# Weight sums of the HGRN's value product: eight VectorE operations replaced by fourteen adding transfers from GpSimd's queue

## The chip, the cores and the metric

The kernel runs on one core of a Trainium2 chip. The metric is the device time of one execution in microseconds. Three runs of the kernel before took 1425.98, 1425.44 and 1424.23 us, median 1425.44 us. Besides these there is one profiled execution, from which all rows of the profile come.

## The reference

A decoder trunk of two layers over 512 tokens of width 1024, in float32. Layer 0 mixes tokens with a Mamba-2 block, layer 1 with an HGRN2 block; after each mixer come a normalisation, a squared-ReLU MLP, a second normalisation and a gated embedding. The change lies at the border of the two layers: the last part of layer 0 and the first product of layer 1.

```
h = layer_norm(ALPHA * x + mix, ...)
h = layer_norm(ALPHA * h + sq_relu_mlp(h, w1, w2), ...)
x = h + sigmoid(h @ ple_w_gate) * (p @ ple_w_proj)
...
q, fz, v, g = split(x @ w_in, 4)      # HGRN2 of layer 1
```

The product that the change is about makes half of the columns of `v` and `g` from `x` and the matching half of the weights.

## The kernel before

**How a product is made.** Each float32 operand is split into a rounded part `hi` and the rest `lo`, and a product takes three matmuls (`mm3`: hi by hi, hi by lo, lo by hi). A weight unit is 128x1024, 512 KB. `unit` loads it into one of three `raw` buffers, `split` makes `whi` (a cast on ScalarE, L113) and `wlo` (a subtraction on VectorE, L115); there are six buffers of each. A `raw` buffer is free for the next load when its `wlo` is done.

**Block products.** The MLP's second product and the first HGRN product multiply 2x2 blocks with seven block products in place of eight. For four of the seven the weight is a sum of blocks, `t1` to `t4`, each of two units. `weight_sums` loads blocks from HBM into eight buffers `r` (L321, on SyncE's queue) and makes sums in place on VectorE (L327 `t3`, L329 `t1`, L330 `t2`, L333 `t4`), two of each per call. In this scheme the sums are, with blocks w11 to w22 of the weights: t3 = w22 - w12, t1 = w12 - w11, t2 = t3 + w11, t4 = w21 - t2.

**The stage around the change.** `mlp_and_gate(0, ...)` ends with the last group of block products (the seven products run in the order a11, s3, s2, a22, s1, a12, s4). After the fifth of them two row chunks of the accumulator are normalised (`layer_norm`: row mean L212, squares on ScalarE L215, L218, square root L219, reciprocal L221, and the two passes L223 and L224 on VectorE), after the seventh the other two. `transpose_split` then transposes each chunk on TensorE (L233, two groups of four transposes a chunk into one PSUM bank `pt`) and evicts it (L237 on ScalarE, L238 on VectorE). The gate's product follows, with weights `wp` (one unit, the projection) and `wg` (four units) for each half, and its own transposes for the next layer (L448, L451 to L453).

`values4` is the first product of the HGRN. Its weight sums are asked for at its beginning, with a priority that puts their instructions ahead in the queues (`VALUE_SUMS`); its matmuls run after the gate's. It uses t3, then t2, t4 and t1. The data side of the blocks is made by `put` on ScalarE and VectorE; the results are drained from PSUM by `first` (a copy on ScalarE) and `more` (an addition on VectorE) into `res`.

**What sets the order.** A scheduler gives each engine one fixed order of instructions from priorities and its own estimates; in `values4` and the HGRN TensorE's order is the written one. SyncE's queue issues in order: each load waits for its buffer, and all loads behind it wait too. Before the change GpSimd issues no transfers and does a few memsets, the last of them (in the line after `scbs`) for the HGRN's score tiles.

Of the kernel before, what the change touches and what calls it, by code (L numbers as in the profile page):

```python
# [11 lines left out]
AF = mybir.ActivationFunctionType  # L12
ALU = mybir.AluOpType
PSUM = bass.MemoryType.PSUM

P = 128
# [18 lines left out]

JOBS = "q2 q3 q4 q5 v2 q6 q7 v3 o".split()
FILL = (2.94, 1.03, 1.27, 1.83, 2.22)
VALUE_SUMS = 60
AHEAD = 6.0
LAST = 0.78  # L40
CONSTS = dict(ident=P, triu=P, eps=1, convw=96, convb=24, dskip=16, snw=16, dtc=2, hlb=8, hnw=1)
# [3 lines left out]
def trunk(ctx: ExitStack, tc, a):  # L45
    nc = tc.nc
# [21 lines left out]
    def mk(p, shape, tag, dt=F32, **kw):  # L68
        return p.tile(list(shape), dt, tag=tag, name=nm(tag), **kw)

    def f32(t):
        return t.bitcast(F32)
# [16 lines left out]
    def tmp(tag, shape, dt=F32):  # L89
        return mk(phase[0], shape, tag, dt, bufs=phase[2].get(tag, 1))  # L90

    def bank(p, tag):
        return mk(p, [P, T], tag)
# [8 lines left out]
    def unit(src, lead=LEAD):  # L102
        n = src.shape[1]
        with tc.high_priority(offset=lead):
            raw = mk(raws, [P, 1024], "raw")
            nc.sync.dma_start(raw[:, :n], src)
        return split(raw[:, :n], lead)

    def split(f, lead=LEAD):
        n = f.shape[1]  # L110
        with tc.high_priority(offset=lead):
            hi = mk(whip, [P, 1024], "whi", F32R)
            nc.scalar.copy(hi[:, :n], f)  # L113
            lo = mk(wlop, [P, 1024], "wlo", F32R)
            nc.vector.tensor_sub(lo[:, :n], f, f32(hi[:, :n]))  # L115
        return hi, lo

    def mm3(out, sh, sl, mh, ml, start, stop, **kw):
        nc.tensor.matmul(out, sh, mh, start=start, stop=False, **kw)  # L119
        nc.tensor.matmul(out, sh, ml, start=False, stop=False, **kw)  # L120
        nc.tensor.matmul(out, sl, mh, start=False, stop=stop, **kw)  # L121
# [26 lines left out]
    with tc.high_priority(offset=FIRST):  # L148
        idle = tmp("sq", [P, T])
        nc.vector.memset(idle, 0.0)  # L150
        ps = bank(psm, "pm")
# [163 lines left out]
    def weight_sums(w, lead, eng=nc.vector):  # L315

        t = [[None, None] for _ in range(4)]

        def load(i, u, src):
            t[i][u] = tmp("r", [P, 1024])  # L320
            nc.sync.dma_start(t[i][u], src)  # L321

        with tc.high_priority(offset=lead):
            for u in range(2):
                load(0, u, w[0][1][u])
                load(2, u, w[1][1][u])
                eng.tensor_sub(t[2][u], t[2][u], t[0][u])  # L327
                load(1, u, w[0][0][u])
                eng.tensor_sub(t[0][u], t[0][u], t[1][u])  # L329
                eng.tensor_add(t[1][u], t[2][u], t[1][u])  # L330
            for u in range(2):
                load(3, u, w[1][0][u])
                eng.tensor_sub(t[3][u], t[3][u], t[1][u])  # L333
        return t
# [171 lines left out]
    def values4(xs, rows, late):  # L506

        w = [[[a["whvg"][4 * j + 2 * i + u] for u in range(2)] for j in range(2)] for i in range(2)]
        t1, t2, t3, t4 = weight_sums(w, VALUE_SUMS, nc.vector)
        a11, a12, a21, a22 = (rows[i][:, j] for i in range(2) for j in range(2))  # L510
        res = [[mk(w4, [P, 2, T], "ab"[i]) for i in range(2)] for _ in range(2)]

        def put(f):
            t = mk(b8, [P, 2, 4, 256], "b8", F32R)
            nc.scalar.copy(t[:, 0], f)
            nc.vector.tensor_sub(t[:, 1], f, f32(t[:, 0]))
            return lambda k, c: tuple(t[:, i, k, c * P : (c + 1) * P] for i in range(2))

        def part(i, j):
            sl = lambda c: slice((2 * i + c) * P, (2 * i + c + 1) * P)  # L520
            return lambda k, c: (xs.h(4 * j + k, sl(c)), xs.l(4 * j + k, sl(c)))

        def product(x, us, banks, start, drain):
            for c in range(2):
                for k in range(4):
                    hi, lo = us[k // 2]
                    ks = slice(k % 2 * T, (k % 2 + 1) * T)
                    mm3(banks[c], *x(k, c), hi[:, ks], lo[:, ks], start and k == 0, k == 3, skip_group_check=True)
                with tc.high_priority(offset=SOON):
                    drain(c, banks[c])  # L530

        def first(i, j):
            return lambda c, ps: nc.scalar.copy(res[j][i][:, c], ps)

        def more(i, j):
            return lambda c, ps: nc.vector.tensor_add(res[j][i][:, c], ps, res[j][i][:, c])

        pair = lambda: [bank(psj, "pj") for _ in range(2)]
        sums = lambda t: [split(v) for v in t]
        x, z, y = [bank(psy, "py%d" % c) for c in range(2)], pair(), pair()  # L540
        with tc.high_priority(offset=EARLY):
            nc.vector.tensor_sub(a11, a11, a21)
            s3 = put(a11)
        product(part(0, 0), [unit(v) for v in w[0][0]], x, True, first(0, 0))
        for f in late:
            f()
        product(part(0, 1), [unit(v) for v in w[1][0]], z, True, more(0, 0))
        nc.vector.tensor_add(a21, a21, a22)
        nc.vector.tensor_sub(a22, a22, a11)
        s2 = put(a22)  # L550
        product(s3, sums(t3), y, True, first(1, 1))
        s1 = put(a21)
        product(s2, sums(t2), x, False, first(1, 0))
        nc.vector.tensor_sub(a12, a12, a22)
        s4 = put(a12)
        product(part(1, 1), sums(t4), y, False, more(1, 0))
        product(s1, sums(t1), x, False, more(1, 1))
        product(s4, [unit(v) for v in w[1][1]], x, False, first(0, 1))
        for j in range(2):
            for i in range(2):  # L560
                g = res[j][i][:, :, 256:]
                nc.scalar.activation(g, g, AF.Silu)
            made["vg", j] = res[j]


    ps = bank(psj, "pj")
    first = [bank(psy, "py0"), bank(psy, "py1"), bank(psj, "pj"), bank(psj, "pj")]
    for k in range(8):
# [10 lines left out]
        parts = [[v[:, k % 2, i * P : (i + 1) * P] for v in four[k // 2]] for i in range(4)]  # L579
# [203 lines left out]
    for j in range(17):  # L783
# [6 lines left out]
        if pend is not None:  # L790
            i = j - 1
# [7 lines left out]
            w = snw[:, i : i + 1]  # L799
# [16 lines left out]
    with tc.manual_schedule(engines={mybir.EngineType.PE}):  # L816
        values4(x_s, rows, late)
# [286 lines left out]
    with tc.manual_schedule(engines={mybir.EngineType.PE}):  # L1104
        for h in range(0, 8, 2):
# [5 lines left out]
            scale = 1.0 if h < 6 else LAST  # L1111
# [129 lines left out]
```

## Time and profile before

| | us |
|---|---|
| median of three runs | 1425.44 |
| the profiled execution | 1424.0 |
| its span on the core | 1422.2 |
| TensorE busy | 1412.7 |
| VectorE busy | 1055.1 |
| ScalarE busy | 754.2 |
| GpSimd busy | 1.9 |

Times in the rows are microseconds from the start of the span. A row of a group gives line, engine, operation, output and inputs, count, busy time and the mean of one in ns, then idle time before it and what ended it. A row of the timeline gives start, length, engine, line, operation, count and, in square brackets, how long the engine was idle before and what released it. `raw<-in_w` is a load into a raw buffer, `r<-in_whvg` a load for the sums of `values4`.

### The profile page before, as it was taken

The page shows a single profiled execution, that of the slowest core. Times are in us where ns is not written, and L with a number is a line of the kernel's source. Part 1 is how long each engine was busy: PE and PEld are TensorE (multiplying, and loading weights), DVE is VectorE, ACT ScalarE, POOL GpSimd, SP SyncE. Part 2 cuts the span into 40 slices and gives each one's busy share as a digit, 9 for nine tenths or more (in the row PEclk, how much of TensorE's full clock was granted, in tenths as well). Part 3 has the DMA queues.
Part 4 walks back from the last instruction along what each step waited for, and adds up shares of the span by engine and source line. Part 5 has one row for each costly group of instructions (what it writes and reads, how often), then busy time and mean ns, then how long its engine had stood idle before and what let it go on. Part 6 is the DMA issues. An engine that isn't in the chain of part 4 may idle for free.

```text
span 1422.2 us, 20042 instructions
## 1 busy us (share of the span) xinstructions
PE 1412.7 (99%) x7869; PEld 1172.5 (82%) x7869; DVE 1055.1 (74%) x1736; ACT 754.2 (53%) x1134; POOL 1.9 (0%) x12
## 2 busy tenths in 40 slices
PE   9999999999999999999999999999999999999998
PEld 7888888888888888888888888877898888888887
DVE  8998687797966767677986576678695867667873
ACT  7776454563265454545545556655555444544641
POOL 0000000000000000000000000000000000000000
PEclk9999999999999999999999999999999999999999
DMA  8432323233333434344621421222163444434231
GB/s 313 138 124 90 120 87 121 102 115 127 145 119 120 161 133 149 133 146 166 214 83 49 133 90 60 75 90 90 46 236 104 148 140 142 149 133 163 89 119 45
DMA packets 49390, 178.00 MB, mean 125 GB/s; under 512 B 5520, under 2 KB 6288, under 8 KB 49168
## 3 DMA queue, kind: packets, MB, share of 16 engines
q1 hardware_dynamic: 49296, 176.73, 36.3%
q8 instruction: 62, 1.02, 0.3%
q14 instruction: 32, 0.26, 0.1%
HBM read 174.54 MB, written 2.16 MB: 124 GB/s over the span
## 4 chain that ended last, share of the span: by engine, by line
PE 94%; DVE 2%; ACT 2%; DMA 1%; issue 0%; ACTq 0%; DVEq 0%
PE pj L119 24%; PE pj L120 24%; PE pj L121 24%; PE py L119 5%; PE py L121 5%; PE py L120 5%; PE py L735 1%; PE pt L233 1%; PE py L741 1%; PE pm L705 1%; DMA raw<-in_wssd 1%; PE py L972 1%; PE pt L693 1%; PE py L1078 1%; DVE wlo L115 0%
## 5 line engine op out<-in xcount | busy, mean ns | idle before, releaser
L113 ACT CAST whi<-raw 128x1024 fp32r<-128x1024 f32 x222 | 232.9, 1051 | 323.5 <-PE pj L120 225.1
L119 PE MATMUL pj<-b,whi 128*128 128x512 f32 (+1 forms) x1006 | 382.3, 381 | 0.7 <-ACT b L237 0.7
L120 PE MATMUL pj<-b,whi 128*128 128x512 f32 (+1 forms) x1006 | 380.3, 378 | 0.0
L121 PE MATMUL pj<-b,wlo 128*128 128x512 f32 (+1 forms) x1006 | 379.3, 377 | 0.0
L115 DVE TENSOR_TENSOR wlo<-raw,whi 128x1024 fp32r<-128x1024 f32 x222 | 270.0, 1221 | 126.4 <-ACT whi L113 124.6
L119 PEld LDWEIGHTS pj<-b,whi 128*128 128x128 f32 x1006 | 188.8, 188 | 34.2 <-ACT b L237 0.9
L121 PEld LDWEIGHTS pj<-b,wlo 128*128 128x128 f32 x1006 | 189.1, 188 | 33.7
L120 PEld LDWEIGHTS pj<-b,whi 128*128 128x128 f32 x1006 | 189.2, 188 | 32.8 <-issue 0.9
L119 PE MATMUL pj<-whi,b 128*128 128x512 f32 x536 | 213.0, 398 | 0.0
L121 PE MATMUL pj<-whi,b 128*128 128x512 f32 x544 | 212.9, 392 | 0.0
L120 PE MATMUL pj<-wlo,b 128*128 128x512 f32 x536 | 210.2, 392 | 0.0
L121 PEld LDWEIGHTS pj<-whi,b 128*128 128x128 f32 x544 | 102.1, 188 | 21.0
L119 PEld LDWEIGHTS pj<-whi,b 128*128 128x128 f32 x536 | 100.7, 188 | 20.7 <-ACT b L1099 0.6
L120 PEld LDWEIGHTS pj<-wlo,b 128*128 128x128 f32 x536 | 100.8, 188 | 19.3
L113 ACT CAST whi<-r 128x1024 fp32r<-128x1024 f32 x72 | 75.8, 1053 | 67.7 <-PE pj L121 38.6
L115 DVE TENSOR_TENSOR wlo<-r,whi 128x1024 fp32r<-128x1024 f32 x72 | 87.7, 1220 | 20.6 <-ACT whi L113 19.9
L121 PE MATMUL py<-whi,b 128*128 128x512 f32 (+1 forms) x250 | 97.0, 388 | 0.0
L120 PE MATMUL py<-wlo,b 128*128 128x512 f32 x224 | 87.1, 389 | 0.0
L119 PE MATMUL py<-whi,b 128*128 128x512 f32 x224 | 87.1, 390 | 0.0
L121 PEld LDWEIGHTS py<-whi,b 128*128 128x128 f32 x250 | 46.9, 188 | 9.7
L634 DVE SCALAR_TENSOR_TENSOR cv<-pj,cst,cv 128x509 f32<-128x509 f32 (+2 forms) x66 | 48.7, 745 | 3.5 <-ACT cv L631 2.8
L119 PEld LDWEIGHTS py<-whi,b 128*128 128x128 f32 x224 | 42.0, 188 | 9.1 <-DVE sg L494 0.3
(292 smaller groups left out, 1850.8 us busy)
## 6 DMA issues: line engine op xcount, KB each, us to landing
raw<-in_w SPq DMA_DIRECT2D x112, 512.0 KB, 3.7
r<-in_w SPq DMA_DIRECT2D x64, 512.0 KB, 4.1
raw<-in_wssd SPq DMA_DIRECT2D x36, 512.0 KB, 3.8
a<-csd SPq DMA_DIRECT2D x16, 512.0 KB, 3.7
raw<-in_wso SPq DMA_DIRECT2D x16, 512.0 KB, 3.6
raw<-in_wg SPq DMA_DIRECT2D x16, 512.0 KB, 3.7
raw<-in_whq SPq DMA_DIRECT2D x16, 512.0 KB, 3.8
raw<-in_whvg SPq DMA_DIRECT2D x14, 512.0 KB, 3.7
```

The costliest lines, as they stand in the source:

```text
L113: nc.scalar.copy(hi[:, :n], f)
L115: nc.vector.tensor_sub(lo[:, :n], f, f32(hi[:, :n]))
L119: nc.tensor.matmul(out, sh, mh, start=start, stop=False, **kw)
L120: nc.tensor.matmul(out, sh, ml, start=False, stop=False, **kw)
L121: nc.tensor.matmul(out, sl, mh, start=False, stop=stop, **kw)
L233: nc.tensor.transpose(pt[:, j * P : (j + 1) * P], src[:, k * P : (k + 1) * P], ident)
L634: nc.vector.scalar_tensor_tensor(cv[:, d:], ps[:, : T - d], convw[:, i, k : k + 1], cv[:, d:], ALU.mult, ALU.add)
L693: nc.tensor.transpose(pt[:, c * P : (c + 1) * P], xs[:, c * P : (c + 1) * P], ident)
L705: nc.tensor.matmul(pst_[:, c * P : (c + 1) * P], btok[:, c, :], xw[:, c].rearrange("p h q -> p (h q)"), start=True, stop=True)
L735: nc.tensor.matmul(yd[64 * r : 64 * r + 64, sl], xdt[:, 2 * c + r, :], m[:, r, sl], start=True, stop=True)
L741: nc.tensor.matmul(yo[:, c * P : (c + 1) * P], pv[:, c - 1].rearrange("p h q -> p (h q)"), cm[:, c * P : (c + 1) * P], start=True, stop=True,)
L972: nc.tensor.matmul(pcs[r][bs, n * c : n * c + n], kk[r][:, ts], qs, start=True, stop=True)
```

## The change

The signs of t1 to t4 are changed so that each is a plain sum: t3 = w12 + w22, t2 = w12 + w22 + w11, t4 = w12 + w22 + w11 + w21, t1 = w11 + w12. The first block of each is loaded by SyncE as before (eight plain transfers, two units for each of four sums). Each further block is added to the tile by a transfer that accumulates, issued from GpSimd's queue: two for t3, four for t2, six for t4, two for t1, fourteen in all, 512 KB each. An addition waits for the load or the addition before it on the same tile. No VectorE operation is left in the sums. The other signs are made up for on the data side: a21, a22 and a12 are formed with other signs, `first` drains with a factor of -1 for half of the results, and `more` subtracts for that half. `VALUE_SUMS` goes from 60 to 120.

```diff
-VALUE_SUMS = 60
+VALUE_SUMS = 120
...
-        t1, t2, t3, t4 = weight_sums(w, VALUE_SUMS, nc.vector)
+        t1, t2, t3, t4 = ([tmp("r", [P, 1024]) for _ in range(2)] for _ in range(4))
+        with tc.high_priority(offset=VALUE_SUMS):
+            for t, parts in ((t3, "12 22"), (t2, "12 22 11"), (t4, "12 22 11 21"), (t1, "11 12")):
+                for u in range(2):
+                    for n, ij in enumerate(parts.split()):
+                        src = w[int(ij[0]) - 1][int(ij[1]) - 1][u]
+                        if n:
+                            nc.gpsimd.dma_start(t[u], src, accum_op=ALU.add)
+                        else:
+                            nc.sync.dma_start(t[u], src)
...
-            return lambda c, ps: nc.scalar.copy(res[j][i][:, c], ps)
+            return lambda c, ps: nc.scalar.activation(res[j][i][:, c], ps, AF.Copy, scale=-1.0 if j else 1.0)
...
-            return lambda c, ps: nc.vector.tensor_add(res[j][i][:, c], ps, res[j][i][:, c])
+            add = nc.vector.tensor_sub if j else nc.vector.tensor_add
+            return lambda c, ps: add(res[j][i][:, c], res[j][i][:, c], ps)
...
-        nc.vector.tensor_add(a21, a21, a22)
-        nc.vector.tensor_sub(a22, a22, a11)
+        nc.vector.tensor_sub(a21, a22, a21)
+        nc.vector.scalar_tensor_tensor(a22, a11, -1.0, a22, ALU.mult, ALU.subtract)
...
-        nc.vector.tensor_sub(a12, a12, a22)
+        nc.vector.scalar_tensor_tensor(a12, a12, -1.0, a22, ALU.mult, ALU.subtract)
```

In the built program the order of instructions differs from before only between the end of layer 0's MLP and its gate (and by the replaced operations). The loads of `r` keep their places in SyncE's queue and wait for the same VectorE instructions. On TensorE the same matmuls and transposes stand in another order: the groups of L233 come some matmuls later. VectorE's order around the normalisation of the first two chunks, from the last product's weights on, with lines numbered as before and the sums marked:

```
before: sum t3, sum t3, wlo, wlo, drain, drain, sum t1, wlo(wp), mean 0, wlo(gate 1), drain,
        L218 0, L223 0, mean 1, L221 0, drain, L224 0, wlo(gate 2), wlo(gate 3), L218 1, L223 1, L221 1, drain, L224 1
after:  wlo, drain, wlo, drain, mean 0, drain, wlo(wp), wlo(gate 1), mean 1, L218 0, L223 0, drain,
        L218 1, L223 1, wlo(gate 2), wlo(gate 3), L221 0, L221 1, drain, L224 0, L224 1
```

On ScalarE, after the change, the casts for gate 2 and gate 3 stand ahead of the two square roots (L219), and the casts of the fourth gate unit and of the next `wp` ahead of the first eviction (L237).

## The prediction

> **What bounds the kernel now.** The first thing to read is the page's busy time against the span.
>
> ```profile
> span 1422.2 us, 20042 instructions
> ...
> PE 1412.7 (99%) x7869; PEld 1172.5 (82%) x7869; DVE 1055.1 (74%) x1736; ACT 754.2 (53%) x1134; POOL 1.9 (0%) x12
> ```
>
> TensorE works 1412.7 of 1422.2 us, so its idle time, some 9.5 us in all, is the most that any change off TensorE can win; VectorE, from which work is taken, has 26% of the span free. The next view is the busy time by stretches, around the place where the eight sums are made (columns: length, then busy us and count of TensorE, weight loads, VectorE, ScalarE and GpSimd, the granted TensorE clock, the DMA engines' share, GB/s).
>
> ```profile
> 680.00:700.00 20.00, 20.00 (x90) 16.55 (x89) 19.79 (x30) 10.84 (x16) 0.00 (x0) 1.00 0.71 237
> 700.00:720.00 20.00, 20.00 (x101) 16.54 (x100) 20.00 (x33) 11.91 (x24) 0.00 (x0) 1.00 0.36 116
> 720.00:740.00 20.00, 20.00 (x99) 16.48 (x98) 16.96 (x21) 10.77 (x16) 0.00 (x0) 1.00 0.25 83
> 740.00:760.00 20.00, 20.00 (x95) 16.55 (x94) 7.85 (x12) 5.85 (x11) 0.00 (x0) 1.00 0.11 40
> ...
> 830.00:1300.00 470.00, 467.37 (x3137) 387.69 (x3136) 340.06 (x646) 249.89 (x455) 0.00 (x0) 1.00 0.34 118
> 1300.00:1422.00 122.00, 118.30 (x542) 97.54 (x541) 77.95 (x113) 50.96 (x75) 0.00 (x0) 1.00 0.28 95
> ```
>
> From 680 to 760 us TensorE is busy 20.00 of every 20 us at clock 1.00. VectorE is full there (19.79 and 20.00 of 20 us), yet nothing on TensorE waits for it. So this stretch has nothing to give back, and all that can happen to the time is that TensorE starts to wait. The DMA engines are at 0.71 of their time between 680 and 700 us. The second look therefore goes to what TensorE would wait for, the transfers and the order on VectorE and ScalarE.
>
> **What is taken away.** The group view of VectorE from 676 to 730 us shows the eight sums and the work beside them.
>
> ```profile
> L115 DVE TENSOR_TENSOR wlo<-raw,whi 128x1024 fp32r<-128x1024 f32 x11 | 13.3, 1221 | 0.2 <-ACT whi L113 0.2
> ...
> L224 DVE SCALAR_TENSOR_TENSOR acc<-acc,lnrs,b 128x1024 f32<-128x1024 f32 x4 | 5.1, 1278 | 0.0
> L223 DVE SCALAR_TENSOR_TENSOR acc<-acc,lnmv,a 128x1024 f32<-128x1024 f32 x4 | 5.1, 1277 | 0.0
> ...
> L362 DVE CUSTOM_DVE_ANT_0 acc<-pj,acc 128x512 f32<-128x512 f32 x4 | 2.7, 678 | 0.0
> L329 DVE TENSOR_TENSOR r<-r,r 128x1024 f32<-128x1024 f32 x2 | 2.4, 1220 | 0.0
> L330 DVE TENSOR_TENSOR r<-r,r 128x1024 f32<-128x1024 f32 x2 | 2.4, 1218 | 0.0
> L333 DVE TENSOR_TENSOR r<-r,r 128x1024 f32<-128x1024 f32 x2 | 2.4, 1216 | 0.0
> L327 DVE TENSOR_TENSOR r<-r,r 128x1024 f32<-128x1024 f32 x2 | 2.4, 1218 | 0.0
> ```
>
> Two each of L327, L329, L330 and L333, eight in all at 1.22 us, 9.8 us of VectorE. None stands ahead of a waiting matmul, so their removal is worth 0 on TensorE. If TensorE were not full there, they would be worth up to 9.8 us; the stretch rows exclude it. The change at `a22` and `a12` from a plain addition to a two-operation form costs 1.28 instead of 1.22 us by the L223 row (128x1024, three operands), two times, hidden since TensorE waits for nothing in the stage that uses them; uncovered it would be 0.1 us. The drains keep their count and size: a copy becomes a copy with a scale, an addition a subtraction; I take 0 for both.
>
> **What is added.** Eight plain loads stay on SyncE's queue and fourteen adding transfers of 512 KB, 7.3 MB, come on GpSimd's queue. The eight plain loads now:
>
> ```profile
> 658.28 8.87 SPq L321 DMA_DIRECT2D r<-in_whvg  x3
> 668.03 0.33 SPq L196 DMA_DIRECT2D b<-in_ln  x1
> 669.17 11.11 SPq L321 DMA_DIRECT2D r<-in_whvg  x5
> 681.08 2.66 SPq L106 DMA_DIRECT2D raw<-in_w  x2
> 684.66 0.33 SPq L106 DMA_DIRECT2D raw<-in_wp  x1
> 689.27 6.59 SPq L106 DMA_DIRECT2D raw<-in_wg  x4
> ```
>
> They start when VectorE has read the old contents of their buffers, the last at 679.9 us, and in the changed program each stands at the same place of the queue behind the same VectorE instruction, so they start as before. The adding transfers follow each load's landing, so from about 662 us. When are their results wanted?
>
> ```profile
> 686.82 1.05 ACT L113 CAST whi<-raw 128x1024 fp32r<-128x1024 f32 x1 [3.45 <-DMA raw<-in_w]
> 688.34 1.05 ACT L113 CAST whi<-raw 128x1024 fp32r<-128x1024 f32 x1 [0.47 <-DMA raw<-in_w]
> ...
> 694.31 0.72 ACT L215 ACTIVATE sg<-acc,lnmv 128x512 f32<-128x512 f32 x1
> ...
> 763.94 1.05 ACT L113 CAST whi<-r 128x1024 fp32r<-128x1024 f32 x1 [0.32 <-PE pj L121]
> ...
> 777.25 1.05 ACT L113 CAST whi<-r 128x1024 fp32r<-128x1024 f32 x1 [0.30 <-PE pj L121]
> ```
>
> The first sum (t3) is read at 763.94 us; the second unit of t4, which takes three additions one behind the other, is read at 777.25. Its first load has landed at about 680 us, so three in a row have some 96 us, 32 us each. If instead all fourteen went one after the other from 662 us, they would have 8.2 us each until 777.25. No row of this trace shows an adding transfer. The nearest rows are plain ones of the same size (median us from issue to landing):
>
> ```profile
> r<-in_whvg SPq DMA_DIRECT2D x8, 512.0 KB, 4.3
> ...
> b<-in_xw SPq DMA_DIRECT2D x2, 512.0 KB, 9.2
> ```
>
> The quiet load lands in 4.3 us, and the one that stands in the crowd at the start of the kernel in 9.2. By either row a chain of three is over by 710 us. So the sums are in time, and GpSimd's memsets, queued behind them, wait for VectorE's later work anyway. I cost the lateness of the sums at 0 and keep it as a rival.
>
> The Trainium skill, DMA: Bandwidth & Descriptors, section Anatomy of one DMA, gives 2.0 us plus bytes over 436 GB/s for a plain transfer from this queue, an estimate of 3.2 us here; the landing row says 4.3 for the other queue, no run so far shows this one, and by either the sums are in time.
>
> **What is moved.** This is where I find the price. Without the eight sums the scheduler has put the other VectorE and ScalarE work into another order, and TensorE's transposes of the first normalised rows (L233) further back. Now they stand here:
>
> ```profile
> 698.43 0.39 PE L119 MATMUL py<-whi,blk 128*128 128x512 f32 x1
> ...
> 701.16 0.60 PE L233 MATMUL pt<-cst,acc 128*128 128x128 f32 x4
> ```
>
> Twelve of the last block product's 24 matmuls come before the first four transposes; in the changed program all 24 do, so TensorE reaches them at 698.43 + 24 x 0.2275 (twelve in 701.16 - 698.43) = 703.9 us. What they wait for is L224 of the first row chunk, and ahead of it there now stand, on ScalarE, the casts of the second and third gate weights before the square root, and on VectorE their two `wlo` subtractions before L224. Following the changed order with the durations above, and loads that land as now:
> - the second cast of the last product's weights starts at 688.34, its `wlo` and one drain end at 691.8;
> - row mean, half of the squares (0.72), cast (1.05), other half, cast, `wlo` (1.22): 696.7;
> - on VectorE the second mean, L223 twice (2 x 1.28) with a drain (0.68) and the wait for two more squares: 700.2; two `wlo`: 702.6; square root used, a drain: 703.4; L224: 704.7.
>
> TensorE would wait 704.7 - 703.9 = 0.8 us. The next four transposes, 14 matmuls on, need the eviction of the first, which on ScalarE now stands behind the cast of another late weight: another 0.2. That is 1.0 us with nothing crowded, the lower bound.
>
> With crowded loads it grows, because the same chain now contains casts that wait for transfers. Three raw buffers only; each next load starts when a `wlo` ends. If loads land in 9.2 us, the second weight of the last product (issued at 683.4) is there at 692.6, the third gate weight (issued when the first projection weight's `wlo` ends, 698.9) at 708.1, L224 ends at 712.5: 8.6 us, and 2.1 at the second group, 10.7. How near are we to which? Between 680 and 700 us the engines moved 237 GB/s at 0.71 of their time, so 334 GB/s at full share. About ten of the fourteen additions, 5.2 MB, fall into the time from 670 to 705 us and cost at least 15.7 us of all engines; free are 0.29 x 20 = 5.8 us between 680 and 700 and 0.64 x 20 = 12.8 between 700 and 720. They barely fit as plain traffic, and do not if they cost twice. I take a landing midway, 6.75 us: the second weight at 690.2, the chain to 696.6, the third gate weight at 703.3, L224 at 707.9, a wait of 4.0; at the second group 1.8. **Sum: 0 - 0 + 4.0 + 1.8 = 5.8 us.** Profiled execution 1424.0 (span 1422.2 and 1.8 around it) gives 1429.8; the median of the runs is 1.4 above it, so 1431.2.
>
> **The rivals.**
> - *No crowding.* The queues fit into each other and only the order costs: +1.0, 1426.4, not slower by what can be told. For it: 0.36 of share after 700. It decides if loads land in under 5.5 us.
> - *Full crowding.* The additions occupy the engines for the whole stretch. At half of 334 GB/s a load takes 3.1 us in its queue; seven issued between 675.2 and 684.7 then land up to 7.7 us late and the same chain gives a wait of about 11, 1436; if an addition costs two plain transfers, a third of the rate, 4.7 us a load, about 18, 1443. Against it: each addition waits for a load and for the one before, so GpSimd's queue is not always full.
> - *Sums late.* Additions that follow each other at 9.2 us each end at 662 + 14 x 9.2 = 791 instead of 777.25: +13.5, 1439. Decides from 8.2 us each. Against it: they overlap, several being under way.
> - *Faster.* VectorE's earlier finish lets later work close TensorE's gaps. These are 2.6 us in 830 to 1300 and 3.7 after 1300, so at most 6.3, 1419. Against it: everything after 760 starts from a TensorE that had no gap, so nothing there can start sooner.
> - *Not what it says.* The scheduler could have put the sums back on VectorE's path; the changed order has none of them there.
>
> By the Trainium skill, DMA: Bandwidth & Descriptors, section SWDGE vs HWDGE vs iDMA, each DMA engine takes turns between the queues that GpSimd feeds and those that SyncE feeds. By that rule full crowding is the case, at 1436. The trace of before has one data queue alone and cannot show it.
>
> **How the numbers follow.** Forecast 0.40, no crowding 0.23, full crowding 0.22, sums late 0.10, faster 0.05. Under 0.2%, 2.85 us, a measurement of this kernel cannot be told from no change. Faster by more: 0.05. Within: the no-crowding case and a little of the forecast's lower end, 0.25. Slower: 0.70. The time is that of the likeliest, 1431.2. The range goes from just under no crowding (1425) to the end of full crowding (1443).
>
> **What would show it.** Right: TensorE idle before L233 near 704 us, released by L224, and before the second L233, released by its eviction; ScalarE's casts between 686 and 712 released by transfers; landings of `raw` there near 7 us; first cast of `r` not waiting for its transfer. No idle before L233 would make the order's cost wrong; a cast of `r` that waits for GpSimd's queue would make the sums late; landings near 4 us with a wait over 3 us would mean another cause. A TensorE wait in another place than 680 to 730 us would make the whole working wrong.

## The result, and the profile after

| | before | after |
|---|---|---|
| median of the runs, us | 1424.94 | 1437.96 |
| the profiled execution, us | 1424.0 | 1437.55 |
| its span, us | 1422.2 | 1435.8 |

Four runs each (before: the three from above and a fourth, 1424.44). The ratio is 1.009, 95% interval 1.0069 to 1.0112: the changed kernel is 13 us slower. The head of its page:

```profile
span 1435.8 us, 20073 instructions
...
PE 1415.0 (99%) x7869; PEld 1173.5 (82%) x7869; DVE 1046.6 (73%) x1728; ACT 753.7 (52%) x1134; POOL 14.2 (1%) x26
```

VectorE has lost 8.5 us of work, somewhat less than the 9.8 of the eight sums, and the span is 13.6 us longer. The view by stretches of the changed kernel (columns as in the prediction) says where:

```profile
680.00:700.00 20.00, 20.00 (x90) 16.57 (x89) 10.96 (x19) 6.53 (x9) 4.53 (x6) 1.00 1.03 289
700.00:720.00 20.00, 9.53 (x37) 7.35 (x35) 12.85 (x21) 7.67 (x14) 4.34 (x5) 0.74 1.05 275
720.00:740.00 20.00, 19.82 (x103) 16.05 (x103) 15.66 (x26) 10.51 (x21) 0.00 (x0) 1.00 0.41 121
```

TensorE is busy for 9.53 of the 20 us from 700 to 720; before it was busy for all of them. The DMA engines, which stood at 0.71 and 0.36 in the first two stretches, are full (1.03 and 1.05; the share counts the time of all packets and comes out a little above 1 where both queues are busy). VectorE and ScalarE have idle time now, so the amount of work on neither of them is what TensorE waits for in the end. Its waits from 690 to 730 us (total, times, longest):

```profile
PE pt L233 <- DVE acc L224: 10.5, 1, 10.5
PE pt L233 <- DVE b L238: 0.2, 1, 0.2
```

One wait of 10.5 us at the first transposes, at the place that the prediction named. What is behind L224 is read from three views: the landings of two loads, the second weight of the last block product (issued in 683 to 684 us) and the third gate weight (issued in 700 to 701.2 us); ScalarE's timeline up to the square root (L219); and VectorE's at L224 itself:

```profile
raw<-in_w SPq DMA_DIRECT2D x1, 512.0 KB, 10.8
...
raw<-in_wg SPq DMA_DIRECT2D x1, 512.0 KB, 9.6
```

```profile
694.49 1.06 ACT L113 CAST whi<-raw 128x1024 fp32r<-128x1024 f32 x1 [0.98 <-DMA raw<-in_w]
...
710.37 1.04 ACT L113 CAST whi<-raw 128x1024 fp32r<-128x1024 f32 x1 [2.66 <-DMA raw<-in_wg]
711.32 0.47 ACT L219 ACTIVATE lnsd<-lnmv,cst 128x1 f32<-128x1 f32 x2
```

```profile
713.32 2.48 DVE L224 SCALAR_TENSOR_TENSOR acc<-acc,lnrs,b 128x1024 f32<-128x1024 f32 x2
```

The second weight takes 10.8 us to land. Behind its cast and its `wlo` come the first row mean, the cast of the projection weight and that weight's `wlo`, which frees the buffer for the third gate weight at 700.7. That one takes 9.6 us, and behind its cast at 710.37 stand the square root and, on VectorE, L224.

The transfers from 670 to 716 us, before (queue: packets, MB, share of 16 engines; then KB and median us from issue to landing):

```profile
q1 hardware_dynamic: 2413, 8.77, 58.8%
...
raw<-in_wg SPq DMA_DIRECT2D x7, 512.0 KB, 3.7
...
raw<-in_w SPq DMA_DIRECT2D x2, 512.0 KB, 5.2
```

and after:

```profile
q0 software_dynamic: 1522, 5.57, 62.3%
q1 hardware_dynamic: 1996, 7.30, 40.9%
...
r<-in_whvg POOLq DMA_DIRECT2D x11, 512.0 KB, 11.0
raw<-in_wg SPq DMA_DIRECT2D x5, 512.0 KB, 9.0
...
raw<-in_w SPq DMA_DIRECT2D x2, 512.0 KB, 11.0
raw<-in_wp SPq DMA_DIRECT2D x2, 512.0 KB, 10.9
```

Loads into `raw` land in 9 to 11 us (medians) in place of 3.7 to 5.2; SyncE's loads of `r`, 4.5 before, take 6.2. The two shares are the key: 5.57 MB of additions took 62.3% of 46 us, 28.7 us of all sixteen engines or 5.15 us for each MB; 7.30 MB of plain loads beside them took 40.9%, 18.8 us or 2.58 us for each MB. Before, 58.8% of 46 us for 8.77 MB make 3.08 us for each MB. So by the packets' time a byte that is added occupied the engines 1.7 to 2.0 times as long as one that is loaded.

### The profile page after: what moved, and what is told of

It reads as the page before. It is cut to its first block, busy times and chain, and to the rows that moved or that the text cites. A ratio compares the mean times of both kernels' runs of the same rounds, so it can differ in the third digit from the quotient of the medians.

```text
span 1435.8 us, 20073 instructions
## 1 busy us (share of the span) xinstructions
PE 1415.0 (99%) x7869; PEld 1173.5 (82%) x7869; DVE 1046.6 (73%) x1728; ACT 753.7 (52%) x1134; POOL 14.2 (1%) x26
## 3 DMA queue, kind: packets, MB, share of 16 engines
q0 software_dynamic: 2016, 7.34, 2.6%
## 4 chain that ended last, share of the span: by engine, by line
PE 89%; DVE 4%; DMA 3%; ACT 2%; issue 1%; SPq 0%; ACTq 0%; DVEq 0%
PE pj L119 23%; PE pj L120 23%; PE pj L121 23%; PE py L119 5%; PE py L120 5%; PE py L121 5%; DVE wlo L115 1%; PE py L745 1%; PE py L751 1%; DMA raw<-in_w 1%; PE pm L715 1%; ACT whi L113 1%; PE pt L233 1%; DMA raw<-in_wp 1%; DMA raw<-in_wssd 1%
## 5 line engine op out<-in xcount | busy, mean ns | idle before, releaser
L119 PE MATMUL pj<-b,whi 128*128 128x512 f32 (+1 forms) x1006 | 382.3, 381 | 0.7 <-ACT b L237 0.7
L119 PEld LDWEIGHTS pj<-b,whi 128*128 128x128 f32 x1006 | 188.9, 188 | 34.5 <-ACT b L237 0.9
L119 PE MATMUL pj<-whi,b 128*128 128x512 f32 x536 | 213.0, 398 | 0.0
L119 PEld LDWEIGHTS pj<-whi,b 128*128 128x128 f32 x536 | 100.8, 188 | 20.7 <-ACT b L1109 0.6
L115 DVE TENSOR_TENSOR wlo<-r,whi 128x1024 fp32r<-128x1024 f32 x72 | 87.7, 1220 | 20.2 <-ACT whi L113 19.3
L119 PE MATMUL py<-whi,b 128*128 128x512 f32 x224 | 87.1, 390 | 0.0
L119 PEld LDWEIGHTS py<-whi,b 128*128 128x128 f32 x224 | 42.0, 188 | 9.1 <-DVE sg L494 0.3
## 6 DMA issues: line engine op xcount, KB each, us to landing
r<-in_whvg POOLq DMA_DIRECT2D x14, 512.0 KB, 10.8
```

## The experiments

The theory at this point: the additions fill the DMA engines, the gate's weights land late, and their casts stand ahead of L224 in the changed order. Rivals: the order alone; the volume of the transfers alone, added or not; and that a place with more room would hide the additions. All ratios are against the kernel before on the same chip.

**Without the additions.** Edit:

```diff
-                            nc.gpsimd.dma_start(t[u], src, accum_op=ALU.add)
+                            continue
```

> Leaves out the fourteen adding transfers; t1 to t4 then hold one weight block each. The order of the instructions on TensorE, VectorE, ScalarE and SyncE is that of the changed kernel. Theory (crowding: the adding transfers make the plain loads late, and the casts that wait for those loads stand ahead of L224): loads of raw land near 4 us again, the wait at the first L233 is 0 to 1.5 us, and the time is 1424 to 1427, as the uncrowded case of the prediction had it (1426.4). Rival (the order alone: the casts of the gate weights stand ahead of L224, whatever the loads do): the wait stays near 10.5 us and the time near 1438.

Ratio 0.9999 (0.999 to 1.0008), as the theory had it. TensorE does not wait at all between 660 and 720 us:

```profile
700.00:720.00 20.00, 20.00 (x98) 16.13 (x98) 18.56 (x30) 11.70 (x24) 0.00 (x0) 1.00 0.43 144
```

The order, the signs and the missing VectorE work together cost nothing. The whole loss belongs to the fourteen transfers.

**The same bytes, not added; and half the bytes.** Edits:

```diff
-                            nc.gpsimd.dma_start(t[u], src, accum_op=ALU.add)
+                            nc.gpsimd.dma_start(t[u], src)
```

```diff
-                            nc.gpsimd.dma_start(t[u], src, accum_op=ALU.add)
+                            nc.gpsimd.dma_start(t[u][:, :512], src[:, :512], accum_op=ALU.add)
```

> The fourteen transfers are plain loads of the same 512 KB from GpSimd's queue, so the sums hold their last block alone. Order unchanged. Theory (the additions occupy the engines about 1.75 times as long per byte as plain loads: 197 against 345 GB/s at full share): with plain loads the share between 680 and 700 us is at or just under 1.0, raw lands in 6 to 8 us, the wait at the first L233 is 3 to 7 us, the time 1428 to 1433. Rival (the volume alone): landings of 9 to 11 us and 1436 to 1439 as with additions. Rival (a second queue and what GpSimd does for it, whatever the bytes): the same, 1438.

> The fourteen adding transfers take half of the columns, 256 KB each; the other half of each sum holds one block alone. Order unchanged. Theory (crowding by engine time): half of the added engine time, so about the same as plain loads of full size: raw lands in 5.5 to 8 us, the wait at the first L233 is 2 to 6 us, time 1427 to 1432. Rival (the number of transfers, the way each is issued or its fixed part, counts, not its bytes): 1436 to 1438. Rival (the order alone): 1438.

Ratios 1.0048 (1.0034 to 1.0062) and 1.0046 (1.0032 to 1.0059), 6.8 and 6.6 us: half of the loss each time. The waits lie in the ranges that the theory gave, the times (1433.24 and 1432.97) just above theirs. TensorE's wait and the transfers from 660 to 720 us, first with plain loads:

```profile
PE pt L233 <- DVE acc L224: 5.2, 1, 5.2
```

```profile
q1 hardware_dynamic: 2901, 10.52, 49.3%
q0 software_dynamic: 2016, 7.34, 31.8%
...
r<-in_whvg POOLq DMA_DIRECT2D x14, 512.0 KB, 6.3
...
raw<-in_wg SPq DMA_DIRECT2D x7, 512.0 KB, 5.7
```

and with half additions:

```profile
PE pt L233 <- DVE acc L224: 5.9, 1, 5.9
```

```profile
q0 software_dynamic: 2016, 3.67, 36.9%
```

7.34 MB loaded plainly took 31.8% of 60 us, 19.1 us of all engines or 2.60 for each MB, no more than SyncE's loads beside it (2.81). So the second queue takes no extra engine time for a byte. 3.67 MB of additions took 22.1 us, 6.0 for each MB. The amount moved says the same without the packets' time: from 680 to 700 us, with the engines full in both kernels, 390 GB/s were moved here and 289 in the changed kernel:

```profile
680.00:700.00 20.00, 20.00 (x90) 16.55 (x89) 12.45 (x20) 6.66 (x10) 4.24 (x8) 1.00 1.01 390
```

In these four kernels the wait follows the engine time, not the bytes nor the number of transfers (fourteen in each of the last three):

| kernel | engine time of GpSimd's queue, 660 to 720 us | wait at the first L233 |
|---|---|---|
| no additions | 0 | 0 |
| plain loads | 19.1 | 5.2 |
| half additions | 22.1 | 5.9 |
| as changed (57.4% of 60) | 34.4 | 10.5 |

In the plain run the transfers of both queues were slow: SyncE's gate weights from 3.7 to a median landing of 5.7 us, and GpSimd's loads took 6.3. This is what the rule of the Trainium skill, DMA: Bandwidth & Descriptors, section SWDGE vs HWDGE vs iDMA, makes one expect (an engine takes turns between the two). The trace agrees with it, with these landings.

**The order of the first rows put right, the additions left.** The normalisation of the first two row chunks gets a priority that puts L219 and L224 of the first chunk ahead of the casts of the gate's weights, as before the change:

```diff
-            with tc.high_priority(offset=SOON if c < 2 or i % 2 == 0 else 0):
+            with tc.high_priority(offset=400 if i == 1 and c < 2 else SOON if c < 2 or i % 2 == 0 else 0):
```

> All fourteen additions as in the changed kernel, but the square root and L224 of the first rows have a higher priority, so that they stand ahead of the casts of the gate weights on ScalarE and VectorE, as before the change. Theory (order and crowding act together; without crowding this order cost nothing): the first L233 no longer waits for a late gate weight; the wait there falls from 10.5 to 0 to 3 us, but the gate weights themselves are still late by 5 us each, so TensorE waits for a wlo some matmuls later, in all 2 to 8 us: time 1428 to 1434. Rival (the order of these few instructions is the whole cause): the time of before, 1424 to 1427. Rival (crowding alone, the order doesn't matter): 1437 to 1439.

Ratio 1.0101 (1.0087 to 1.0115): no gain. Our theory gave 1428 to 1434 and is refuted in this part; the rival with crowding alone was nearest. The waits from 690 to 730 us, and two loads from the chain:

```profile
PE py L119 <- DVE lnsum L362: 6.3, 3, 4.5
PE pt L233 <- DVE acc L224: 2.5, 1, 2.5
```

```profile
684.25 12.38 DMA raw<-in_w
...
704.13 7.90 DMA raw<-in_wg
```

The wait at L233 falls to 2.5 us, but TensorE then waits 6.3 us at products (L119), for VectorE's L362, the drain of an earlier product. The chain of the longest of these waits goes back from L362 over the normalisation of the second chunk, whose squares on ScalarE stand behind the cast of a late gate weight (7.90 us), to the second weight of the last block product (12.38 us). The waits are 8.8 us in all, and twice the matmuls behind them run slowly (see the last section), which by the timeline adds some 4 us more. So the same late loads hold TensorE in another place, and moving the first rows alone gains nothing. Whether an order exists in which late loads cost less, this run doesn't show: other work still stands behind their casts.

**The same volume added beside the order of before.** In the kernel before, 28 additions of 256 KB into a spare tile, one behind the other:

```diff
+        extra = tmp("extra", [P, 512])
...
+            nc.gpsimd.tensor_copy(extra, r[:, :512])
+            for n in range(28):
+                nc.gpsimd.dma_start(extra, w[n // 2 % 2][n // 4 % 2][n // 14][:, n % 2 * 512 : (n % 2 + 1) * 512], accum_op=ALU.add)
```

> The kernel before, whole, with 28 adding transfers of 256 KB (7.3 MB, one behind the other) into a spare tile, which nothing reads, from about 662 us on. The order on the engines is that of before. Theory (crowding makes the gate weights late under the order of before too, though L224 doesn't stand behind their casts): raw lands in 7 to 11 us between 670 and 716; the first L233 waits 0 to 2 us, TensorE waits for casts of gate weights after it; time 1428 to 1436. Rival (only the changed order is sensitive): 1424 to 1427. Rival (crowding alone sets it): 1436 to 1440, as in the changed kernel.

Ratio 1.0017 (1.0008 to 1.0026), 2.4 us, just below the theory's 1428 to 1436. One addition at a time, they are spread over 140 us and more; only 2.36 MB of it fell between 660 and 720 us, 24.6% of the engines, and TensorE waited 0.9 us there, at a product and not at L233. The gate's weights landed in 4.3 us, where the theory had 7 to 11: this run did not make the crowd that it was meant to make. Order and pace both differ from the changed kernel here, so this run alone doesn't part them. The next one keeps the changed order.

**One addition at a time in the changed kernel.**

```diff
+            gate, prev = mk(sm, [P, 16], "gate"), None
...
+                            if prev is not None and n == 1:
+                                nc.gpsimd.tensor_scalar(gate[:, :1], prev[:, :1], 0.0, None, ALU.mult)
+                                nc.gpsimd.tensor_add(t[u][:, :1], t[u][:, :1], gate[:, :1])
                             nc.gpsimd.dma_start(t[u], src, accum_op=ALU.add)
+                            prev = t[u]
```

> All fourteen additions of 512 KB as in the changed kernel, but the first addition of each sum waits (through a tiny GpSimd addition of a zero made from the sum before) until the sum before it is complete, so that one is under way at a time. Order on TensorE, VectorE and ScalarE as in the changed kernel. Theory (what counts is how many additions are under way beside a plain load; 28 smaller ones in a row cost the kernel before 2.4 us only): raw lands in 5 to 7 us between 670 and 716, the wait at the first L233 is 0 to 4 us, time 1426 to 1431; the last additions end near 662 + 14 x 6.5 = 753 us, in time. Rival (the sum of the added engine time counts, however it is spread): 1435 to 1439. Rival (in a row they are late): a cast of r waits for GpSimd's transfer at 764 to 778 us, 1432 or more.

Ratio 1.0053 (1.004 to 1.0067), 7.6 us, above the range that the theory gave and below that of the engine time alone (1435 to 1439). The waits of the stage are as it said:

```profile
PE pt L233 <- DVE acc L224: 1.6, 1, 1.6
PE pt L233 <- DVE b L238: 0.9, 1, 0.9
```

From 660 to 720 us GpSimd's queue took 33.7% of the engines, 20.2 us, and the wait at the first L233 was 1.6 us; the plain loads with 19.1 us had 5.2. So the table above is not the whole rule: the same engine time costs less when the transfers do not crowd together. The last addition was issued at 765.5 us and no cast of `r` waited. The waits explain 2.5 of the 7.6 us; the run with a tile alone (below) accounts for part of the rest.

**The additions held back until the gate's weights are in.** A gate made from the late rows, near 730 us, in three forms. In the first each sum's gate reads the rows:

```diff
+        gate, late_col = mk(sm, [P, 1], "gate"), rows[0][:, 0, 0, :1]
...
+                        if n == 1:
+                            nc.gpsimd.tensor_scalar(gate, late_col, 0.0, None, ALU.mult)
+                            nc.gpsimd.tensor_add(t[u][:, :1], t[u][:, :1], gate)
```

In the second they are read once:

```diff
+                            if not held:
+                                held.append(nc.gpsimd.tensor_scalar(gate, late_col, 0.0, None, ALU.mult))
```

In the third (gated_16) they are read once too, the tile has 64 bytes, and all gates stand ahead of the additions:

```diff
+            gate = mk(sm, [P, 16], "gate")
+            nc.gpsimd.tensor_scalar(gate[:, :1], rows[0][:, 0, 0, :1], 0.0, None, ALU.mult)
+            todo = []
...
-                            nc.gpsimd.dma_start(t[u], src, accum_op=ALU.add)
+                            todo.append((t[u], src))
...
+                    nc.gpsimd.tensor_add(t[u][:, :1], t[u][:, :1], gate[:, :1])
+            for dst, src in todo:
+                nc.gpsimd.dma_start(dst, src, accum_op=ALU.add)
```

> The changed kernel with its result, but the first adding transfer of each sum waits (by a GpSimd addition of a zero made from the late rows) until the second L452, near 728 us, so that nothing is added while the gate weights are loaded. Order on the other engines unchanged. Theory (crowding between 670 and 716 us): wait at the first L233 0 to 1.5 us, time as without the additions, 1424 to 1427, provided that the sums still come in time for their casts at about 764 to 778 us: fourteen transfers of 3.9 us (the quietest landing) one after the other would end near 728 + 55 = 783, so a wait of a few us at the last cast would not surprise, none at the first. Rival (the adding transfers cost the same wherever they stand, or the order alone does): 1436 to 1440.

> As the gated kernel, but the late rows are read once, at the first gate: in the gated kernel each of the eight gates read them, and VectorE's L556, which overwrites them, waited for the last gate and so for the additions. Theory (crowding while the gate weights load): no wait at L233 nor at L448, the time 1424 to 1428 as without additions; a wait of up to 3 us where the additions end near 773 us and the last weight of t4 is wanted near 777 is allowed, and so is a late load of whvg among them. Rival (fourteen additions cost about 13 us wherever they stand): 1436 to 1440, with a TensorE wait of 8 us or more in 740 to 790 us.

> As gated_once, but the gate's tile takes 64 bytes of each partition instead of 4, so that the tiles allocated after it keep their alignment. In both gated kernels the matmuls outside the stage of the change ran slower than in the others (0.9 us in 480 to 640, 1.3 us in 1117 to 1388). Theory (the tile of 4 bytes shifted the tiles behind it): no such drift, the time is 1 to 4 us above before, from the late transfer of lmask among the additions (a wait of about 2 us at L530): 1426.5 to 1430. Rival (the drift comes of the gating or of the chip's state): as gated_once, 1431 to 1434.

In all three the wait at L233 is gone. The first missed by far, at 1.0098 (1.0084 to 1.0112), through the experiment itself: its gates read the rows that VectorE overwrites, and the last gates waited for additions (waits of all engines from 730 to 800 us):

```profile
DVE blk L556 <- POOL gate L517: 16.0, 1, 16.0
...
PE pt L448 <- DVE b L453: 8.6, 1, 8.6
```

Read once, it gave 1.0045 (1.0032 to 1.0058), 1432.64 us, between the ranges of the theory and of the rival; with the larger tile it gave 1.0032 (1.0021 to 1.0043), 1431.33 us, above the theory's range and in the rival's. What TensorE still waits for is shown in the second by VectorE's timeline, the transfers from 728 to 790 us and TensorE's waits:

```profile
779.27 0.29 DVE L839 CAST lmask<-raw 128x256 uint8<-128x256 f32 x1 [5.13 <-DMA raw<-in_lmask]
```

```profile
raw<-in_whvg SPq DMA_DIRECT2D x6, 512.0 KB, 9.6
...
raw<-in_lmask SPq DMA_DIRECT2D x1, 128.0 KB, 9.7
```

```profile
PE py L121 <- DVE b L530: 1.7, 1, 1.7
```

Moved by 70 us, the same additions make other loads late. The loads of `whvg` have slack there. A load of only 128 KB takes 9.7 us (3.2 without additions), VectorE waits 5.13 us for it with `wlo` subtractions behind, and TensorE 1.7. That is the only wait of TensorE that they leave in the place with room.

**A tile of 4 bytes and nothing else.** The gated kernels and the one with single additions lost time far from the stage. The run without additions, with the tile added:

```diff
+        gate = mk(sm, [P, 1], "gate")
+        nc.gpsimd.memset(gate, 0.0)
```

> No adding transfers (as no_adds; t1 to t4 hold one block each), but one tile of 4 bytes for each partition, set by a GpSimd memset, is allocated where the gated kernels have theirs. Theory (that tile shifts the ones behind it and slows their matmuls): the same drift, 0.9 us in 480 to 640 and 1.3 us in 1117 to 1388, time 1427.5 to 1430 where no_adds had the time of before. Rival (the tile does nothing): within 0.1% of before.

Ratio 1.0015 (1.0006 to 1.0023), 2.1 us. The distance of two casts on ScalarE's timeline, without the tile:

```profile
458.70 1.05 ACT L113 CAST whi<-r 128x1024 fp32r<-128x1024 f32 x1 [1.02 <-PE py L121]
...
639.35 1.05 ACT L113 CAST whi<-raw 128x1024 fp32r<-128x1024 f32 x1 [3.64 <-PE pj L120]
```

and with it:

```profile
458.26 1.05 ACT L113 CAST whi<-r 128x1024 fp32r<-128x1024 f32 x1 [1.01 <-PE py L121]
...
639.84 1.06 ACT L113 CAST whi<-raw 128x1024 fp32r<-128x1024 f32 x1 [3.67 <-PE pj L120]
```

180.65 us against 181.58, long before the stage of the change. So the tile with its memset is enough for the drift, without any gating. In the profiled executions the five kernels that have such a tile take 181.49 to 181.59 us there, the other eight 180.65 or 180.66, the changed kernel among them. Those with 64 bytes drift by 0.8 us too, so the explanation by alignment, in the form that it was tried, falls; why a tile does this stays open. Against the kernel with the tile, on the same chip, held back additions cost 1431.33 - 1428.59 = 2.7 us and single ones 1433.53 - 1428.59 = 4.9 us, where all at once cost 13. Of these the waits above explain 1.7 and 2.5 us; the rest was not followed further.

**The signs alone.** The sums on VectorE, with plus signs, and all edits of the data side:

```diff
+        sub = eng.tensor_add if plus else eng.tensor_sub
...
-                eng.tensor_sub(t[2][u], t[2][u], t[0][u])
+                sub(t[2][u], t[2][u], t[0][u])
...
+        t1, t2, t3, t4 = weight_sums(w, VALUE_SUMS, nc.vector, True)
```

> The plus signs and the edits of the data side (subtracting drains, two-operation forms) with the sums on VectorE as before; no adding transfer. The order on the engines is that of before. Theory (these edits cost 0): ratio to before within 0.999 to 1.001. Rival (the signed evictions or two-operation forms cost on TensorE's path): 1428 or more.

Ratio 1.0002 (0.9993 to 1.001). They cost nothing.

No run pointed to a version that beats the kernel before: with the additions gone altogether, and the VectorE work of the sums too, the time is that of before.

## Why the prediction was right or wrong

- *What bounds the kernel; the sums' removal is worth 0; sums in time; drains and two-operation forms at 0:* right. The runs without additions and with the signs alone are both within 0.1% of before, and no cast of `r` waited for GpSimd's queue even with one addition at a time.
- *The place and the chain:* right. TensorE waits before the first L233, released by L224, behind casts that wait for transfers.
- *The order's own cost, 0.8 + 0.2 us:* measured 0. The run without additions has this order and no wait in the stage; L224 of the first chunk ends there about as the first transposes start, at 704.9 us, so the chain is just in time.
- *The landing of 6.75 us, "midway":* this is the step that failed. The loads into `raw` of that stage had median landings of 9.0 to 11.0 us, and the two that the prediction's chain runs over, the second weight and the third gate weight, took 10.8 and 9.6, so the wait at the first L233 was 10.5 and not 4.0. The chain itself holds: its working with 9.2 us for both had 8.6, and 1.6 and 0.4 us more make 10.6. The prediction had the test in hand (the additions "barely fit as plain traffic, and do not if they cost twice") and then split the difference between two cases, where the term is not a mean of anything. Plain loads of the same volume already cost 6.8 us, about the forecast's 5.8; the additions took up to twice their engine time, 5.15 against 2.58 us for each MB, and the engines were full from 670 to 716 us.
- *The rival of full crowding:* its account, engines occupied for the whole stretch, is the right one, but its two prices were not both near. 1436, nearly the time, assumed that an addition costs one plain transfer, and with transfers at that cost the run took 1433. For additions that cost two it had a wait of 18 us and 1443, too much. So the nearness of 1436 is in part luck.
- *The second group, 1.8 us:* measured 0.2. That the long first wait gave the later loads time is likely, but no run parts it.
- *A term that was missing:* after the long wait the matmuls ran slowly (below), 1.6 us more.
- *Sum:* a mark behind the stage (a group of transposes at L448) moved from 743.19 to 756.08 us, 12.9; of this 10.5 + 0.2 are waits and 1.6 the slow matmuls, and 0.6 is not assigned. The forecast was 5.8. The direction was right, the time lies in the range, and the size is off by more than a factor of two.
- *Whether the order matters once the loads are late:* the prediction wrote the loss as one of the changed order, made worse by crowding. The run with the first rows put right shows that this part of the order is not needed for the loss: the late weights stop TensorE elsewhere. That the whole order of before would lose as much under the same crowd is not shown; the run meant for it (28 small additions) did not make that crowd.

## What to carry to other kernels

An adding transfer in place of a vector operation is no free work: here it took the DMA engines 1.7 to 2 times as long for each byte as a plain load, and the loads into `raw` beside it took two to three times as long to land, a small one of 128 KB in the gated run too. Ask which loads share the time, how long the chain is that reuses few buffers behind them, and add up engine time (bytes, up to twice for additions) against what is free, before asking whether the sum itself is in time. If it must be done, let one addition follow another, or start them when no chained load is under way; here that cut the cost of 13 us to some 5 and 3, and neither gained on the sums on VectorE.

## What the runs showed of the hardware that was not expected

After a long wait TensorE is slow for a while. TensorE's timeline in the changed kernel (starts in the first column):

```profile
703.79 0.39 PE L121 MATMUL py<-whi,blk 128*128 128x512 f32 x1
714.65 1.12 PE L233 MATMUL pt<-cst,acc 128*128 128x128 f32 x4 [10.47 <-DVE acc L224]
715.42 0.78 PE L119 MATMUL pj<-whi,a 128*128 128x512 f32 x1
...
717.28 0.63 PE L120 MATMUL pj<-wlo,a 128*128 128x512 f32 x1
717.70 0.58 PE L121 MATMUL pj<-whi,b 128*128 128x512 f32 x1
718.12 0.40 PE L119 MATMUL pj<-whi,a 128*128 128x512 f32 x1
718.35 0.40 PE L120 MATMUL pj<-wlo,a 128*128 128x512 f32 x1
```

and after the shorter wait of the kernel with one addition at a time:

```profile
708.42 0.66 PE L233 MATMUL pt<-cst,acc 128*128 128x128 f32 x4 [1.61 <-DVE acc L224]
708.84 0.48 PE L119 MATMUL pj<-whi,a 128*128 128x512 f32 x1
709.15 0.40 PE L120 MATMUL pj<-wlo,a 128*128 128x512 f32 x1
```

Until 718.12 matmuls start 0.42 us apart, from then on 0.23; the granted clock of the stretch is 0.74. From L233 to the seventh matmul behind it it takes 3.47 us, against 1.89 after the short wait: 1.6 us more. The same slow phase, 3.5 to 3.9 us long, follows the waits of 5.2 and 5.9 us with plain and half additions; after 1.6 us there is none. The Trainium skill, TensorE: Matmul & The Clock Gate, Part 1, says that an idle window of about 3.4 us halves TensorE's clock and that about as long a busy one restores it; these rows agree. One case is not told by the length of a single wait: with the first rows put right, waits of 2.5 and 1.4 us with only four transposes between them are followed by 5.3 us of slow matmuls. So here the waits of TensorE of 5 us and more, or shorter ones close together, cost more than their length.
